# Feed-forward sums moved from GpSimd to VectorE, with a replanned order

## The chip, the core and the metric

The kernel runs on one core of a Trainium2 chip. The metric is the device time of one execution in microseconds, as a median of runs. The engines are TensorE (PE in the profile; its weight loads are PEld), VectorE (DVE), ScalarE (ACT), GpSimd (POOL) and SyncE (SP), whose queue issues the transfers.

## What is computed

One layer of an encoder trunk over 1024 prompt rows and 32 sample rows (1056 in all), width 1024: a pair of recurrent mixers, cross attention, and a gated feed-forward of width 2816, each added to the running rows x. The end of the layer, cut to what this change touches:

```python
x = x + cross_attend(rmsnorm(x, lw['norm_cross']), mk, mv, lw['w_cq'], lw['w_co'])
n = rmsnorm(x, lw['norm_ffn'])
x = x + (jax.nn.silu(n @ lw['w_ff1']) * (n @ lw['w_ff3'])) @ lw['w_ff2']
```

and after it a final RMSNorm. Everything is float32.

## The kernel before

The program is first recorded as a graph: every call on an engine makes a node (`record`), with the tiles it reads and writes. Then `order` plans all of it. It keeps a clock for each engine, gives each node a duration (`price`), a delay between engines (`wait`) and a priority (the longest path to the end, less the node's `bias`, L382 to L385), picks for each engine the ready node with the earliest start and, among those, the highest priority, and places tiles in SBUF regions and PSUM banks as it goes. `LEAD` says how many nodes of earlier phases may be left when a node of a phase is taken. `emit` then issues all nodes in that order from one line, L340, so nearly every row of the profile has that line, and the tiles' names must tell rows apart: `bank` is PSUM; `rw` holds split weights, `wr` and `ma` raw weights; `f`, `ma`, `mb` and `r` hold the rest. SP issues all transfers, in its own order.

A float32 matrix product is done with two float32r parts for each factor: ScalarE rounds a tile to `hi` (CAST in the profile), another engine subtracts to get `lo`, and three matmuls (hi hi, hi lo, lo hi) are added in PSUM for each 128 of the inner dimension.

The phases that matter here:

- **Cross output** (phase 3, end of `cross`): `w_co` in 8 column tiles of 128, 4 row blocks of 264 each. Behind each block `operands` adds x, scales it, stores x to DRAM, and forms what the feed-forward reads: split tiles and, in the manner of Strassen and Winograd, the sums t1 to t4 of its quarters. It also adds up squares; three matmuls with a matrix of ones and a few small operations then give the row scale `rb`.
- **Hidden layer** (phase 4, `ff_hidden`): 11 column blocks of 256 (m), each with two branches, `w_ff1` and `w_ff3`. A branch is seven products (1 to 7) in place of eight; each is 4 inner tiles x 3 matmuls x 2 row halves (s) of 264 rows, so a branch is 168 matmuls and a block 336. `fast_w` loads the raw weights (512 KB twice), makes four weight sums of 128x512 on GpSimd, and for each product a hi (ScalarE) and a lo (VectorE). `fast` issues the matmuls; products 7 and 4, 2 and 3 share PSUM banks, the second adding onto the first after a VectorE sum (128x264, out of PSUM) has read it. At the end of the first branch (`evac1`) come, on 128x1056 tiles, a product with `rb`, a sigmoid, a product with it, and a second product with `rb`; at the end of the second (`evac3`) the product of both branches and four differences of 128x264 for each row half, then stores to DRAM.
- **Second product** (phase 5, `ff_out`): the first 10 hidden blocks, in groups of `FF_GROUPS` pairs, 2 in each of five groups. For each group the operands are loaded and split (128x528, hi on ScalarE, lo on GpSimd and VectorE in turn), then for each of four column tiles (j) seven products of 12 matmuls for each pair, and VectorE adds each out of PSUM to sums in SBUF: 14 sums of 128x264 for each group and j. In group 2 GpSimd adds x, 128x1056 eight times.
- **Tail** (phase 6): the last hidden block by a plain product, then norm and stores.

Of the kernel before, what the change touches and what calls it, by code (L numbers as in the profile page):

```python
# [20 lines left out]
T = TP + NS  # L21
# [13 lines left out]
FF_GROUPS = (2, 2, 2, 2, 2)  # L35
# [16 lines left out]
WAIT, WAIT_PE, SWITCH = 0.0, 0.1, 0.06  # L52
FREE_PS, FREE_SB = 0.2, 0.2
# [7 lines left out]
LEAD = {0: BIG, 1: 1100, 2: 250, 3: 400, 4: 300, 5: 200, 6: 200}  # L61
HOME = {"keep": ("f0", "r0"), "wr": ("wr",), "wh": ("rw",), "wl": ("rw",), "wr2": ("wr",), "wh2": ("rw",), "wl2": ("rw",),
        "op": ("r0", "mb"), "sr": ("wr", "ma"), "sh": ("rw",), "sl": ("rw",), "sh3": ("rw",), "sl3": ("rw",), "sx": ("ma", "f0"),
# [3 lines left out]
FIFO = {"wr": 2, "wh": 2, "wl": 2, "p": 44, "rp": 5, "op": 56, "sr": 2, "sh": 4, "sl": 4, "sx": 4, "sh3": 8, "sl3": 8, "hst2": 4, "xr": 2, "wr2": 4, "wh2": 8, "wl2": 8, "ckv": 7, "mrow": 2}  # L67
# [119 lines left out]
class Node:  # L187
    def __init__(self, graph, eng):
        self.eng, self.i = eng, len(graph.nodes)
        self.calls, self.cost, self.late = [], 0.0, 0.0  # L190
        self.preds, self.bufs, self.unit, self.bias, self.phase = {}, {}, graph.unit, graph.bias, graph.phase
        graph.nodes.append(self)
# [10 lines left out]
def wait(a, b):  # L203
# [42 lines left out]

def change(a, b):

    if a is None:
        return 0.0  # L250
    (_, x, kx), (m, y, ky) = a.calls[-1], b.calls[0]
# [10 lines left out]
class Graph:  # L262
# [36 lines left out]
    def record(self, eng, method, args, kw):  # L299
# [5 lines left out]
        cost, late = price(eng, method, args, kw)  # L305
# [45 lines left out]
    def order(self):  # L351
# [30 lines left out]
        for n in reversed(nodes):  # L382
            n.path = n.cost + n.late + max((s.path + wait(n.eng, s.eng) for s in succs[n]), default=0.0)
# [3 lines left out]
        clock = dict.fromkeys(engines, 0.0)  # L387
        ready = {e: [] for e in engines}
# [122 lines left out]
        def add(n):  # L511
            t = max((when[p] + wait(p.eng, n.eng) for p in n.preds), default=0.0)
# [5 lines left out]
        while len(done) < len(nodes):  # L518
            turn_over()
            best = None  # L520
            for e in engines:
# [7 lines left out]
                for t, n in sorted(ready[e], key=lambda r: (max(r[0], now), -r[1].path)):  # L529
                    t = max(t, now)  # L530
# [19 lines left out]
            clock[e] = start + n.cost  # L550
            when[n] = start + n.cost + n.late
# [36 lines left out]
class Net:  # L588
# [330 lines left out]
    def cross(self):  # L919
# [76 lines left out]
        for m in range(KD):  # L996
            w = self.load_w(self.i["w_co"][0, :, 128 * m:128 * m + 128], KD)
            self.gemm(w, act, KD, self.operands(m, sq), blocks=[(TQ * q, TQ) for q in range(4)])
        self.rstd(sq)

    def operands(self, m, sq):
# [9 lines left out]
        def evac(t0, n, ps):  # L1011
# [8 lines left out]
            if m >= 4 or h == 0:  # L1020
                self.split(hs, ls, x)
            if m < 4 and h == 1:
                t1 = self.t[5, k, s] = new("t1")
                G.tensor_tensor(t1, x, self.x[k, s, 0], ALU.subtract)
            if m >= 4 and h == 1:
                E = V if m == 7 else G
                t2, t3, t4 = self.t[6, k, s], _, self.t[4, k, s] = new("t2"), new("t3"), new("t4")
                E.tensor_tensor(t3, x, self.x[k, s, 1], ALU.subtract)
                self.split(self.xh[:, k, t0:t0 + n], self.xl[:, k, t0:t0 + n], t3)
                E.tensor_tensor(t2, x, self.t[5, k, s], ALU.subtract)  # L1030
                E.tensor_tensor(t4, self.x[m, s, 0], t2, ALU.subtract)
            if m == 0:
                S.activation(sq[:, t0:t0 + n], t, AF.Square)
            else:
                S.activation(t, t, AF.Square)
                G.tensor_tensor(sq[:, t0:t0 + n], sq[:, t0:t0 + n], t, ALU.add)
        return evac
# [16 lines left out]
    def fast_w(self, ap, nk, order, tags, pairs):  # L1054
# [4 lines left out]
        raw = self.wp.tile([128, nk, 2, 256], F32, tag="sr", name="fraw")  # L1059
        if pairs:  # L1060
            nc.sync.dma_start(raw, ap.rearrange("(k e p) m -> p k e m", e=2, p=128))
        else:
            for e in range(2):
                nc.sync.dma_start(raw[:, :, e], ap[128 * nk * e:128 * nk * (e + 1)].rearrange("(k p) m -> p k m", p=128))
        a11, a21, a12, a22 = raw[:, :, 0, 0:128], raw[:, :, 0, 128:256], raw[:, :, 1, 0:128], raw[:, :, 1, 128:256]
# [3 lines left out]
        for i in order:  # L1069
# [5 lines left out]
            hi, lo = (self.wp.tile([128, nk, 128], F32R, tag=tag, name="f" + tag[:2]) for tag in tags)  # L1075
# [4 lines left out]
    def fast(self, ws, act, nk, evac, order):  # L1080
# [721 lines left out]
```

## Time and profile before

| | |
|---|---|
| median of 3 runs | 2042.04 us (2041.89 to 2043.87) |
| profiled execution | 2041.77 us, span 2040.0 us |
| TensorE busy | 1892.7 us (93%) |
| VectorE busy | 1431.3 us (70%) |
| GpSimd busy | 910.2 us (45%) |
| ScalarE busy | 944.9 us (46%) |
| granted TensorE clock, mean | 0.972 |

A row of the stage view reads: stretch, its length, then busy time and number of instructions of PE, PEld, DVE, ACT and POOL, the granted clock, the DMA share and GB/s. A row of the timeline reads: start, length, engine, line, operation, out<-in, shape, count, and in brackets the idle time ahead of it with what ended it. A row of groups has busy time and mean ns behind the count. A row of the waits view says who waited for whom: total us, times, longest. Times are from the start of the span. Busy time of VectorE and GpSimd contains what one of them waits for the other, since an instruction that has started counts.

### The profile page before, as it was taken

What the parts mean: (1) busy time and instruction counts of PE and PEld (TensorE: products, weight loads), DVE (VectorE), ACT (ScalarE), POOL (GpSimd) and SP (SyncE); (2) the same over time, 40 slices, a digit from 0 to 9 for tenths busy, and PEclk for the clock granted to TensorE, in tenths of its full rate; (3) what the DMA queues carried; (4) which work ended last, traced back from release to release, by engine and by line L of the source; (5) the groups of instructions that cost most, each with busy time, mean ns of one, the idle gap of its engine ahead of it and who ended that gap; (6) DMA issues with size and microseconds to landing.
All of it is one profiled execution on the core that took longest, in us unless ns stands there. A gap on an engine that the chain in (4) does not pass through costs nothing. (4 is left out here: it accounts for less than half of the span.)

```text
span 2040.0 us, 40406 instructions
## 1 busy us (share of the span) xinstructions
PE 1892.7 (93%) x15377; PEld 1739.6 (85%) x15377; DVE 1431.3 (70%) x3093; ACT 944.9 (46%) x2454; POOL 910.2 (45%) x1159
## 2 busy tenths in 40 slices
PE   7899999998998999899999997999999999899898
PEld 6878777787877788899999987899999999899897
DVE  4876667767767765645654558776777667889996
ACT  5577537845664766633322345323322222463322
POOL 5742343344435331116200056566566556666742
PEclk9999989999999999899999998999999999999999
DMA  4100101011010112541211122123322224465422
GB/s 138 42 22 25 36 23 32 20 31 32 22 32 18 33 33 69 177 137 42 62 42 42 53 75 74 42 95 105 106 79 80 89 80 138 143 197 159 127 84 96
DMA packets 158179, 149.52 MB, mean 73 GB/s; under 512 B 10144, under 2 KB 146464, under 8 KB 157984
## 3 DMA queue, kind: packets, MB, share of 16 engines
q1 hardware_dynamic: 157984, 146.93, 22.8%
q8 instruction: 121, 1.98, 0.4%
q14 instruction: 74, 0.61, 0.1%
HBM read 111.02 MB, written 35.88 MB: 72 GB/s over the span
## 5 line engine op out<-in xcount | busy, mean ns | idle before, releaser
L340 PE MATMUL bank<-r,rw 128*128 128x264 f32 (+1 forms) x5664 | 914.4, 313 | 32.0 <-DVE rw L340 6.1
L340 PEld LDWEIGHTS bank<-r,rw 128*128 128x128 f32 x5664 | 811.2, 191 | 55.3 <-DVE rw L340 9.0
L340 PE MATMUL bank<-mb,rw 128*128 128x264 f32 (+4 forms) x3600 | 505.0, 296 | 50.0 <-DVE ma L340 19.8
L340 PEld LDWEIGHTS bank<-mb,rw 128*128 128x128 f32 x3600 | 478.1, 192 | 61.5 <-issue 26.0
L340 DVE TENSOR_TENSOR f<-bank,f 128x264 f32<-128x264 f32 (+6 forms) x895 | 321.6, 384 | 163.3 <-PE bank L340 148.5
L340 POOL TENSOR_TENSOR f<-f 128x264 f32<-128x264 f32 (+8 forms) x255 | 240.0, 954 | 303.6 <-ACT f L340 237.9
L340 PE MATMUL bank<-f 128*128 128x64 f16 (+6 forms) x2630 | 297.4, 253 | 35.8 <-DVE f L340 16.1
L340 ACT CAST rw<-wr 128x256 fp32r<-128x256 f32 (+2 forms) x223 | 145.5, 660 | 298.1 <-PE bank L340 171.3
L340 DVE TENSOR_TENSOR rw<-wr,rw 128x256 fp32r<-128x256 f32 (+2 forms) x193 | 178.5, 928 | 68.5 <-ACT rw L340 63.3
L340 PEld LDWEIGHTS bank<-f 128*128 128x128 f32 (+4 forms) x1582 | 165.9, 160 | 65.6 <-DVE f L340 17.9
L340 ACT ACTIVATE f<-f 128x256 f32<-128x256 f32 (+7 forms) x374 | 151.4, 422 | 111.5 <-DVE f L340 89.9
L340 ACT COPY f<-f 64x256 f16<-64x256 f16 (+1 forms) x408 | 149.1, 368 | 46.2 <-DVE f L340 37.9
L340 DVE TENSOR_TENSOR f<-f 128x256 f32<-128x256 f32 (+8 forms) x152 | 115.2, 773 | 27.9 <-ACT f L340 14.8
L340 DVE TENSOR_TENSOR rw<-ma,rw 128x512 fp32r<-128x512 f32 (+1 forms) x86 | 115.6, 1356 | 16.7 <-ACT rw L340 15.3
L340 POOL TENSOR_SCALAR f<-f 128x64 f32<-128x64 f32 (+6 forms) x124 | 54.9, 444 | 157.9 <-DVE f L340 98.2
L340 ACT COPY f<-bank 128x264 f32<-128x264 f32 (+6 forms) x221 | 75.7, 362 | 98.9 <-PE bank L340 80.9
L340 ACT CAST rw<-ma 128x512 fp32r<-128x512 f32 (+1 forms) x86 | 50.9, 598 | 138.9 <-PE bank L340 80.8
L340 POOL TENSOR_TENSOR r<-f,r 128x352 fp32r<-128x352 f32 (+1 forms) x41 | 56.1, 1377 | 67.7 <-ACT r L340 38.1
L340 POOL TENSOR_TENSOR rw<-wr,rw 128x1024 fp32r<-128x1024 f32 x30 | 71.7, 2393 | 29.5 <-ACT rw L340 25.9
L340 PEld LDWEIGHTS <-f 128*128 128x128 f16 x1156 | 52.6, 99 | 35.8 <-issue 8.6
L340 ACT ACTIVATE f<-bank,f 128x256 f32<-128x256 f32 (+4 forms) x122 | 51.0, 431 | 61.9 <-DVE f L340 26.1
L340 PE MATMUL bank<-f,mb 64*64 64x64 f32 (+7 forms) x830 | 74.3, 248 | 1.9 <-DVE f L340 1.1
(180 smaller groups left out, 2292.8 us busy)
## 6 DMA issues: line engine op xcount, KB each, us to landing
wr<-in_w_ff_dram SPq DMA_DIRECT2D x40, 512.0 KB
f<-h_scratch SPq DMA_DIRECT2D x62, 264.0 KB
wr<-in_w_in_dram SPq DMA_DIRECT2D x30, 512.0 KB
ma<-in_w_ff_dram SPq DMA_DIRECT2D x24, 512.0 KB
h_scratch<-f SPq DMA_DIRECT2D x19, 528.0 KB
f<-mix_scratch SPq DMA_DIRECT2D x24, 176.0 KB
x_scratch<-f SPq DMA_DIRECT2D x32, 132.0 KB
mb<-in_x_prompt_dram SPq DMA_DIRECT2D x16, 256.0 KB
```

Of the source, the lines that this page charges most:

```text
L340: getattr(eng, method)(*args, **kw)
```

## The change

- In the hidden layer, GpSimd's products with the sigmoid and with `rb`, and its differences behind `evac3`, go to VectorE. GpSimd keeps the sums of weights.
- In the second product, all operand low parts, the additions of x (now in group 1) and the final additions of the common part go to VectorE; the groups are 3, 3, 2, 2 pairs.
- At the end of the cross output, the differences t1, t2, t3 go to VectorE; t4 and its low part are GpSimd's.
- The first hidden block runs both branches in turn: products 1, 2, 7, 3 of each alternating, then 5, 6, 4 of one and of the other, with a PSUM bank for each product above 2, and its own rule for the sums. The load of its first weights belongs to the phase ahead and follows the sixth of the cross weights.
- hi and lo of a weight or operand are one tile.
- From phase 3 on the planner uses other durations (`close_price`) and delays, and a clock for a port: an operation of GpSimd on two tensors, or one of VectorE with two inputs from SBUF, is not started before the last such one ends. Biases are added; `LATER` puts the elementwise end of a branch 10 us back in priority. `LEAD` of phase 4 falls from 300 to 100.

What this does to the order, at three places. Rows are as the built program has them: number, line, operation, out<-in, shape, count. VectorE in a middle column block of the hidden layer, around the end of the first branch, before:

```order
2173 L340 TENSOR_TENSOR f_0_71<-f_0_71 128x1056
2174 L340 TENSOR_TENSOR f_0_71<-bank_61,f_0_71 128x264
2175 L340 TENSOR_TENSOR f_0_71<-f_0_71 128x1056
2176 L340 TENSOR_TENSOR rw_83<-ma_12981,rw_83 128x512 x2
2177 L340 TENSOR_TENSOR f_0_71<-bank_62,f_0_71 128x264
2178 L340 TENSOR_TENSOR f_0_71<-bank_58,f_0_71 128x264
2179 L340 TENSOR_TENSOR rw_83<-ma_12981,rw_83 128x512
2180 L340 TENSOR_TENSOR f_0_71<-f_0_71 128x1056
2181 L340 TENSOR_TENSOR ma_12981<-bank_63,f_0_71 128x264
```

and now:

```order
2246 L415 TENSOR_TENSOR f_0_71<-f_0_71 128x1056
2247 L415 TENSOR_TENSOR f_0_71<-bank_63,f_0_71 128x264
2248 L415 TENSOR_TENSOR f_0_71<-f_0_71 128x1056
2249 L415 TENSOR_TENSOR rw_83<-ma_12947,rw_83 128x512
2250 L415 TENSOR_TENSOR f_0_71<-f_0_71,ma_12947 128x1056
2251 L415 TENSOR_TENSOR f_0_71<-f_0_71 128x1056
2252 L415 TENSOR_TENSOR f_0_71<-bank_61,f_0_71 128x264
2253 L415 TENSOR_TENSOR f_0_71<-f_0_71 128x1056
2254 L415 TENSOR_TENSOR f_0_71<-bank_62,f_0_71 128x264
2255 L415 TENSOR_TENSOR f_0_71<-f_0_71 128x1056
2256 L415 TENSOR_TENSOR ma_12947<-bank_59,f_0_71 128x264
```

The products with the sigmoid (rows 2250 and 2251) and both second products with `rb` (2253 and 2255) stand between sums out of PSUM.

GpSimd over the same column block, now (before, the three rows of 128x1056 and eight of 128x264 stood among them):

```order
631 L415 TENSOR_TENSOR ma_12947<-wr_75 128x512
632 L415 TENSOR_TENSOR ma_12947<-ma_12947,wr_75 128x512
633 L415 TENSOR_TENSOR wr_75<-wr_75 128x4x128
634 L415 TENSOR_TENSOR ma_12947<-ma_12947,f_0_71 128x4x128
635 L415 TENSOR_TENSOR ma_12947<-ma_12947 128x512
636 L415 TENSOR_TENSOR f_0_71<-ma_12947 128x512
637 L415 TENSOR_TENSOR ma_12947<-ma_12947 128x4x128
638 L415 TENSOR_TENSOR wr_75<-wr_75,ma_12947 128x4x128
```

Only the four weight sums of each branch are left.

TensorE at the end of the cross output (`ma_8341` is its last operand) and the start of the hidden layer (`r_0_79`), with the sums of squares (128x352), before:

```order
4288 L340 MATMUL bank_60<-ma_8341,rw_83 128x264 x6
4289 L340 MATMUL bank_58<-r_0_79,rw_83 128x264 x12
4290 L340 MATMUL bank_59<-r_0_79,rw_83 128x264 x12
4291 L340 MATMUL bank_58<-r_0_79,rw_83 128x264 x6
4292 L340 MATMUL bank_61<-f_0_71 128x352
4293 L340 MATMUL bank_63<-f_0_71 128x352
```

and now:

```order
4288 L415 MATMUL bank_65<-ma_8341,rw_83 128x264 x6
4289 L415 MATMUL bank_63<-r_0_79,rw_83 128x264 x6
4290 L415 MATMUL bank_59<-r_0_79,rw_83 128x264 x6
4291 L415 MATMUL bank_63<-r_0_79,rw_83 128x264 x6
4292 L415 MATMUL bank_59<-r_0_79,rw_83 128x264 x6
4293 L415 MATMUL bank_60<-r_0_79,rw_83 128x264 x6
4294 L415 MATMUL bank_61<-r_0_79,rw_83 128x264 x6
4295 L415 MATMUL bank_63<-r_0_79,rw_83 128x264 x6
```

Rows 4289 to 4292 are product 1 of the first branch, 4293 and 4294 begin product 1 of the second, and 4295 product 2 of the first. The sums of squares come 20 rows of six matmuls after the start.

The diff, cut:

```diff
-FF_GROUPS = (2, 2, 2, 2, 2)
+LATER = 10.0
+FF_GROUPS = (3, 3, 2, 2)
...
-LEAD = {0: BIG, 1: 1100, 2: 250, 3: 400, 4: 300, 5: 200, 6: 200}
+LEAD = {0: BIG, 1: 1100, 2: 250, 3: 400, 4: 100, 5: 200, 6: 200}
...
+def close_price(eng, method, args, kw):
...
+        return 0.065 + n * 1.05e-3 + (0.065 if method == "scalar_tensor_tensor" else 0.0), 0.0
...
+    if method == "tensor_tensor":
+        return 0.13 + n * 2.12e-3 + (0.45 if args[3] == ALU.pow else 0.0), 0.0
...
+def shares_port(eng, method, args):
+    if eng == "gpsimd":
+        return method == "tensor_tensor"
+    if eng != "vector" or method not in ("tensor_tensor", "scalar_tensor_tensor", "tensor_tensor_scan", "copy_predicated"):
+        return False
+    return sum(isinstance(v, View) and v.buf.space == "SB" and math.prod(v.shape[1:]) > 1 for v in args[1:]) >= 2
...
+                    t = max(t, now, port) if n.port else max(t, now)
...
+            if n.port:
+                port = clock[e] - (0.15 if e == "gpsimd" else 0.0)
...
+            if m == 5:
+                self.late = nc.nodes[-1]
...
-                G.tensor_tensor(t1, x, self.x[k, s, 0], ALU.subtract)
+                V.tensor_tensor(t1, x, self.x[k, s, 0], ALU.subtract)
-                E = V if m == 7 else G
                 t2, t3, t4 = self.t[6, k, s], _, self.t[4, k, s] = new("t2"), new("t3"), new("t4")
-                E.tensor_tensor(t3, x, self.x[k, s, 1], ALU.subtract)
+                V.tensor_tensor(t3, x, self.x[k, s, 1], ALU.subtract)
                 self.split(self.xh[:, k, t0:t0 + n], self.xl[:, k, t0:t0 + n], t3)
-                E.tensor_tensor(t2, x, self.t[5, k, s], ALU.subtract)
-                E.tensor_tensor(t4, self.x[m, s, 0], t2, ALU.subtract)
+                V.tensor_tensor(t2, x, self.t[5, k, s], ALU.subtract)
+                G.tensor_tensor(t4, self.x[m, s, 0], t2, ALU.subtract)
...
+        if first:
+            nc.phase -= 1
...
+        if first:
+            for node in nc.nodes[-2:]:
+                node.preds[self.late] = None
...
-            hi, lo = (self.wp.tile([128, nk, 128], F32R, tag=tag, name="f" + tag[:2]) for tag in tags)
+            w = self.wp.tile([128, 2, nk, 128], F32R, tag=tag, name="fw")
+            hi, lo = w[:, 0], w[:, 1]
...
+            bank = i if alone and i > 2 else " aadcdbc"[i]
...
+                elif m:
+                    V.tensor_tensor(o[:, {7: 2, 4: 1, 3: 3}[i]], ps, c, ALU.add)
+                elif i == 4:
+                    V.tensor_tensor(o[:, 1], ps, o[:, 1], ALU.add)
+                    V.tensor_tensor(o[:, 1:4], o[:, 1:4], c.unsqueeze(1).to_broadcast([128, 3, TQ]), ALU.add)
                 else:
+                    S.copy(o[:, 2 if i == 7 else 3], ps)
+                    if i == 7:
+                        S.copy(o[:, 1], ps)
+            final = 3 if m else 4
...
+                    nc.bias = self.turn + LATER
...
-                    G.tensor_tensor(t, t, sg, ALU.mult)
-                    (G if s else V).tensor_tensor(th, th, r, ALU.mult)
+                    V.tensor_tensor(t, t, sg, ALU.mult)
+                    V.tensor_tensor(th, th, r, ALU.mult)
...
-                    G.tensor_tensor(y[:, 2], x[:, 3], x[:, 0], ALU.subtract)
-                    G.tensor_tensor(y[:, 0], x[:, 2], y[:, 2], ALU.subtract)
-                    G.tensor_tensor(y[:, 1], x[:, 2], x[:, 3], ALU.subtract)
-                    G.tensor_tensor(y[:, 3], x[:, 1], y[:, 0], ALU.subtract)
+                    V.tensor_tensor(y[:, 2], x[:, 3], x[:, 0], ALU.subtract)
+                    V.tensor_tensor(y[:, 0], x[:, 2], y[:, 2], ALU.subtract)
+                    V.tensor_tensor(y[:, 1], x[:, 2], x[:, 3], ALU.subtract)
+                    V.tensor_tensor(y[:, 3], x[:, 1], y[:, 0], ALU.subtract)
...
+                order = [(f, i) for i in (1, 2, 7, 3) for f in range(2)] + [(f, i) for f in range(2) for i in (5, 6, 4)]
+                jobs = [(self.fast_w(self.i[name][0, :, cs], 4, order, f, "sh", False, f == 0), evac)
+                        for f, (name, evac) in enumerate((("w_ff1", evac1), ("w_ff3", evac3)))]
+                self.fast(jobs, act, 4, order, True)
...
-                    (V if k % 2 else G).tensor_tensor(lo, raw, hi.bitcast(F32), ALU.subtract)
+                    V.tensor_tensor(lo, raw, hi.bitcast(F32), ALU.subtract)
...
-                    (V if n == 2 else G).tensor_tensor(dst, dst, common[j][:, s], ALU.add)
+                    V.tensor_tensor(dst, dst, common[j][:, s], ALU.add)
...
+                w = self.fast_w(self.i["w_ff2"][0, rows, 256 * j:256 * j + 256], n, jobs, 0, "sh3", True)
...
-                if g == 2:
+                if g == 1:
...
-                        G.tensor_tensor(acc[m], acc[m], x, ALU.add)
+                        V.tensor_tensor(acc[m], acc[m], x, ALU.add)
```

More of the change, by code (lines that the diff above doesn't have):

```diff
@@ L191, in __init__ @@
         self.preds, self.bufs, self.unit, self.bias, self.phase = {}, {}, graph.unit, graph.bias, graph.phase
+        self.close, self.port = graph.phase >= CLOSE, False
         graph.nodes.append(self)
@@ L200, in __getattr__, with wait @@
         return lambda *args, **kw: self.graph.record(self.name, method, args, kw)
-def wait(a, b):
+def wait(n, s):
+    a, b = n.eng, s.eng
+    if s.close:
+        return 0.0 if a == b else DELAY.get((a, b), DELAY[a])
     if a == b:
@@ L304, in record @@
         self.open = node if eng == "tensor" else None
-        cost, late = price(eng, method, args, kw)
+        cost, late = (close_price if node.close else price)(eng, method, args, kw)
+        node.port = node.close and shares_port(eng, method, args)
         node.cost, node.late = node.cost + cost, max(node.late, late)
@@ L382, in order @@
         for n in reversed(nodes):
-            n.path = n.cost + n.late + max((s.path + wait(n.eng, s.eng) for s in succs[n]), default=0.0)
+            n.path = n.cost + n.late + max((s.path + wait(n, s) for s in succs[n]), default=0.0)
         for n in nodes:
@@ L387, in order @@
         clock = dict.fromkeys(engines, 0.0)
+        port = 0.0
         ready = {e: [] for e in engines}
@@ L511, in add @@
         def add(n):
-            t = max((when[p] + wait(p.eng, n.eng) for p in n.preds), default=0.0)
+            t = max((when[p] + wait(p, n) for p in n.preds), default=0.0)
             ready[n.eng].append((t, n))
@@ L1052, in halves, with fast_w @@
         return v[:, :, 0], v[:, :, 1]
-    def fast_w(self, ap, nk, order, tags, pairs):
+    def fast_w(self, ap, nk, order, job, tag, pairs, first=False):
         nc = self.nc
@@ L1059, in fast_w @@
         raw = self.wp.tile([128, nk, 2, 256], F32, tag="sr", name="fraw")
+        phase = nc.phase
+        if first:
+            nc.phase -= 1
         if pairs:
@@ L1068, in fast_w @@
         G.tensor_tensor(s2, s1, a11, ALU.subtract)
-        for i in order:
+        for i in [i for f, i in order if f == job]:
             if i == 7:
@@ L1078, in fast_w, with fast @@
             yield hi, lo
-    def fast(self, ws, act, nk, evac, order):
+    def fast(self, jobs, act, nk, order, alone=False):
         nc = self.nc
         ps = {}
-        for i in order:
+        for f, i in order:
+            ws, evac = jobs[f]
+            self.turn += 0.73 * nk
             nc.bias = self.turn
-            self.turn += 0.73 * nk
             hi, lo = next(ws)
-            bank = " aadcdbc"[i]
-            fresh = (bank, 0) not in ps
+            bank = i if alone and i > 2 else " aadcdbc"[i]
+            fresh = (f, bank, 0) not in ps
             for s in range(2):
+                nc.bias = self.turn
                 if fresh:
-                    ps[bank, s] = self.psg.tile([128, TQ], F32, tag="g", name="ps_f")
-                p = ps[bank, s]
+                    ps[f, bank, s] = self.psg.tile([128, TQ], F32, tag="g", name="ps_f")
+                p = ps[f, bank, s]
                 for k in range(nk):
@@ L1129, in ff_hidden @@
             cs = slice(256 * m, 256 * m + 256)
-            order = (1, 6, 7, 5, 4, 2, 3) if m else (1, 2, 7, 5, 3, 6, 4)
-            out, u, full = [[None, None], [None, None]], [None, None], [False, False]
+            out, u = [[None, None], [None, None]], [[None, None], [None, None]]
             def sums(f, i, s, ps):
@@ L1196, in ff_out @@
         order = (1, 6, 7, 5, 2, 4, 3)
+        jobs = [(0, i) for i in order]
         acc = [fp.tile([128, T], F32, tag="ac", name="acc") for _ in range(KD)]
@@ L1229, in ff_out @@
             for j in range(4):
[L1230 to L1232 removed]
+                w = self.fast_w(self.i["w_ff2"][0, rows, 256 * j:256 * j + 256], n, jobs, 0, "sh3", True)
+                self.fast([(w, partial(evac, g, j))], act, n, jobs)
+                if g == 1:
                     for m in (2 * j, 2 * j + 1):
```

107 lines of the change are left out of this document (79 added, 28 removed).

## The prediction

> **What bounds the kernel now.** I read the busy shares first, then the span cut into its stages, then what TensorE waited for in each stage, then one such wait step by step.
>
> ```profile
> PE 1892.7 (93%) x15377; PEld 1739.6 (85%) x15377; DVE 1431.3 (70%) x3093; ACT 944.9 (46%) x2454; POOL 910.2 (45%) x1159
> 975.00:1134.00 159.00, 157.67 (x916) 145.47 (x915) 85.84 (x234) 44.64 (x118) 7.00 (x7) 1.00 0.16 48
> 1134.00:1195.00 61.00, 60.28 (x456) 57.50 (x455) 31.98 (x77) 22.91 (x56) 13.68 (x14) 1.00 0.22 68
> 1195.00:1257.00 62.00, 52.05 (x390) 51.11 (x389) 43.53 (x61) 27.96 (x69) 39.37 (x40) 0.89 0.19 61
> 1257.00:1319.00 62.00, 49.57 (x345) 46.44 (x344) 49.92 (x80) 29.45 (x68) 31.80 (x22) 0.92 0.20 60
> 1319.00:1769.00 450.00, 423.08 (x3363) 417.39 (x3362) 321.30 (x397) 133.64 (x254) 282.43 (x199) 0.98 0.30 100
> 1769.00:1998.00 229.00, 212.46 (x1686) 207.07 (x1685) 218.30 (x423) 96.23 (x241) 141.97 (x131) 1.00 0.44 136
> 1998.00:2040.00 42.00, 32.87 (x215) 28.49 (x213) 26.55 (x51) 11.23 (x36) 9.91 (x30) 0.92 0.28 104
> 1360.00:1380.00 20.00, 20.00 (x167) 20.00 (x166) 10.80 (x17) 4.06 (x9) 10.97 (x11) 1.00 0.20 68
> ```
>
> TensorE is the bound overall. The last row is a stretch without a gap: 20/167 = 0.12 us from matmul to matmul. Against that pace 1195 to 1319 (end of the cross output, first column block of the hidden layer) holds 735 matmuls, 88 us of work in 124, so 36 lost. The other ten hidden column blocks, 1319 to 1769, hold 3363, 403 us in 450: 47 lost. The second product, 1769 to 1998, holds 1686, 202 us in 229: 27 lost. These 110 us are what the change can reach; from 975 to 1195 TensorE has no gap to give. VectorE is busy 218 of 229 us in the second product.
>
> ```profile
> PE bank L340 <- DVE ma L340: 16.6, 8, 2.9
> PE bank L340 <- DVE f L340: 4.7, 2, 2.7
> PE bank L340 <- ACT rw L340: 3.8, 8, 1.0
> PE bank L340 <- DVE rw L340: 1.7, 8, 0.2
> 1476.19 2.79 POOL L340 TENSOR_TENSOR f<-f,ma 128x1056 f32<-128x1056 f32 x1 [6.13 <-ACT ma L340]
> 1476.54 5.86 DVE L340 TENSOR_TENSOR rw<-ma,rw 128x512 fp32r<-128x512 f32 x2
> 1478.94 5.81 POOL L340 TENSOR_TENSOR f<-f 128x1056 f32<-128x1056 f32 x2
> 1483.01 2.29 DVE L340 TENSOR_TENSOR rw<-ma,rw 128x512 fp32r<-128x512 f32 x1
> 1485.23 2.33 DVE L340 TENSOR_TENSOR f<-f 128x1056 f32<-128x1056 f32 x1
> 1487.48 0.42 DVE L340 TENSOR_TENSOR ma<-bank,f 128x264 f32<-128x264 f32 x1
> 1488.05 3.17 PE L340 MATMUL bank<-mb,rw 128*128 128x264 f32 x24 [1.97 <-DVE ma L340]
> 1493.09 0.68 DVE L340 TENSOR_TENSOR rw<-f,rw 128x512 fp32r<-128x512 f32 x1
> ```
>
> The first four rows are TensorE's waits from 1319 to 1769: 26.8 us, 21.3 of them for a VectorE sum out of PSUM. The rest is one of them. GpSimd has three 1056-element products in a row; VectorE's low parts of weights, 0.68 us alone (last row), take 2.93 each until those are through, so the sum of product 7 ends at 1487.90, and product 4, which adds onto the same bank, waits 1.97 us. It comes back once a column block. So operations that read two SBUF tensors on VectorE wait out GpSimd's, one by one; those that read PSUM do not (0.42).
>
> By the Trainium skill (SBUF — State Buffer, "Who interferes with whom") a VectorE instruction with two SBUF inputs and a GpSimd instruction that reads SBUF exclude each other; the 2.93 against 0.68 agrees.
>
> **Steady hidden blocks.** Prices alone, and group means:
>
> ```profile
> 1460.12 1.26 DVE L340 TENSOR_TENSOR ma<-ma,f 128x1056 f32<-128x1056 f32 x1
> 1267.66 0.42 DVE L340 TENSOR_TENSOR f<-f 128x264 f32<-128x264 f32 x1
> 1488.66 1.28 POOL L340 TENSOR_TENSOR wr<-wr 128x512 f32<-128x512 f32 x1
> 1461.46 0.76 POOL L340 TENSOR_TENSOR f<-ma 128x264 f32<-128x264 f32 x1 [5.06 <-DVE ma L340]
> L340 POOL TENSOR_TENSOR f<-f 128x1056 f32<-128x1056 f32 x19 | 54.1, 2869 | 0.0
> ```
>
> One column block is 336 matmuls, 40.3 us. VectorE now: 14 low parts x 0.68, 20 PSUM sums x 0.42, five 1056 products x 1.26: 24.2 us. GpSimd: 8 weight sums x 1.28, 8 differences x 0.76, three products x 2.87: 24.9. The change moves three products and eight differences: VectorE 24.2 + 3 x 1.26 + 8 x 0.42 = 31.3, GpSimd 10.2. Over ten blocks VectorE was busy 321, 32.1 a block: 7.9 us more than its 24.2, waited on GpSimd, 0.32 of GpSimd's 24.9. With the same share VectorE is at 31.3 + 0.32 x 10.2 = 34.6 of 40.3; with every GpSimd operation waited out it is at 41.5, just over TensorE. The first is nearer: the order puts GpSimd's sums singly, and no long product is left in its queue. So TensorE stays the bound. Of the 47 lost, the PSUM waits fall from 21.3 to 4, the weight waits from 5.5 to 4. The clock, mean 0.98, cost 0.02 x 450 = 9.
>
> ```profile
> 1575.00:1579.00 4.00, 2.98 (x14) 3.02 (x15) 2.31 (x6) 1.07 (x2) 2.89 (x2) 0.57 0.00 0
> ```
>
> It halves right behind the longest gaps, as here, so 3 remain; of the other 11, small gaps, 9. That leaves 20: **27 us gained** (10 if every GpSimd operation is waited out, 38 at the floor).
>
> **Second product.**
>
> ```profile
> 1840.43 0.41 DVE L340 TENSOR_TENSOR rw<-wr,rw 128x256 fp32r<-128x256 f32 x1
> L340 DVE TENSOR_TENSOR r<-ma,r 128x528 fp32r<-128x528 f32 x1 | 0.7, 696 | 0.0
> L340 DVE TENSOR_TENSOR f<-bank,f 128x264 f32<-128x264 f32 x162 | 63.9, 420 | 1.0 <-PE bank L340 0.9
> L340 POOL TENSOR_TENSOR r<-f,r 128x528 fp32r<-128x528 f32 x17 | 25.4, 1496 | 9.7 <-ACT r L340 9.7
> L340 POOL TENSOR_TENSOR wr<-wr 128x256 f32<-128x256 f32 x17 | 14.5, 852 | 0.3
> ```
>
> Groups of 3, 3, 2, 2 pairs in place of five of 2 save 56 VectorE sums out of PSUM (240 to 184, 23.5 us), and VectorE takes 35 operand low parts x 0.70, 16 sums x 0.42 and eight 1056 sums x 1.26 of x: 41 us. The first two groups: 8 x 126 matmuls, 121 us. VectorE's order there has about 70 sums x 0.42, 48 operand parts x 0.70, 55 parts of weights of 384 columns (0.55, between 0.41 and 0.68) and a few more: 106; with 0.32 of GpSimd's 32 sums of about 1 us it comes to 116, under TensorE. I take 125. The last two groups: 8 x 84 matmuls, 81 us. VectorE has 112 x 0.42, 51 x 0.41, 13 x 0.70, 18 final sums x 0.42, and five long ones: 91. So here VectorE becomes the bound, 91 + 0.32 x 32 x 0.74 (GpSimd's 256-column sums alone, an estimate from 0.85 contended) = 99. Together 224 against 229: **5 gained** (212 with no waiting, 253 with all).
>
> **Boundary.** Before:
>
> ```profile
> 1257.35 3.10 PE L340 MATMUL bank<-r,rw 128*128 128x264 f32 x24
> 1264.46 1.32 PE L340 MATMUL bank<-r,rw 128*128 128x264 f32 x6 [4.01 <-ACT f L340]
> 1244.20 0.93 SPq L340 DMA_DIRECT2D wr<-in_w_ff_dram  x2
> 1248.30 0.62 ACT L340 CAST rw<-wr 128x512 fp32r<-128x512 f32 x1 [1.38 <-DMA wr<-in_w_ff_dram]
> ```
>
> The stop at 1264 comes after product 1 alone, 24 matmuls. After the change both branches share the first block, so two products 1 stand there and products 5, 6, 4, whose operands come last, follow eight others; the three sum-of-squares matmuls follow 120 matmuls of the feed-forward, not 30. Against that, product 1 of the second branch needs weights whose transfer goes into a region that opens when the cross output has ended: by the rows above 4 us from issue to ScalarE, then 0.62 and 0.68, against 2.9 us of product 1: some 2 to 5 us of stop, and VectorE has a queue of about 25 short operations (10 us) from the last output blocks. VectorE takes 20 differences x 0.42 = 8.4 there and gives GpSimd 8 operand parts; GpSimd loses about as many longer ones. Of 36 lost I take 22: **14 gained** (0 to 24). The first transfer issued a phase early gains nothing: on SP it still stands behind the last cross weights, and behind 23 stores of x where it stood behind 27.
>
> The cross stage is reordered too, since prices change from there; TensorE was full, so 0 (3 either way). The tail gets six more sums: **1 lost**.
>
> Sum: 27 + 5 + 14 - 1 = 45. The profiled execution took 2041.8 us, 1.8 more than its span and 0.3 under the median of the runs: 2042 - 45 = **1997 us**.
>
> **Rivals.** *TensorE's floor*: no term waits, 38 + 17 + 24 - 1 = 78: 1964. For it: VectorE still has 15% free in the hidden blocks. Against: the second product. *VectorE becomes the bound*, since most GpSimd operations are waited out (share 0.8): 31.3 + 8.2 = 39.5 a block still fits, 22 gained; the second product 106 + 26 and 91 + 19 = 242, 13 lost; boundary 8: 2042 - 16 = 2026. For it: VectorE at 218 of 229 there already. *Nothing gained*: both engines' work is one queue at the port, whichever of them does it (share 1): hidden 10, second product -24, boundary 14: 2042. The rows speak against it, as the work halves on its way (2.87 to 1.26, 0.76 to 0.42). By the Trainium skill (Perfetto Trace Analysis, "Optimizing Scalar/DVE Operations") moving work between GpSimd and VectorE might not help, as they share a read port; no run here shows it yet. *Slower*: GpSimd starves at the port. Its chain of four weight sums a branch waits each time for a 1.26 product, weights are late, TensorE waits 2 x 1.26 in each of 22 blocks: 55 us over the forecast's gain of 45, and ten halved clock stretches at 1.7: 2042 - 45 + 55 + 17 = 2069. It decides from 45/22 = 2 us a block. Against it: GpSimd is free three quarters of the time, and weights are ordered several products ahead.
>
> **How the numbers follow.** Forecast 0.50, floor 0.20, VectorE bound 0.18, nothing 0.06, slower 0.06. Range 1966 to 2030: the floor's edge and the VectorE case with 4 to spare; the last two and the extreme of the floor stay out. Differences under 0.2% (4 us) count as no change here: faster 0.88, same 0.06, slower 0.06.
>
> **What would show it.** Right: no 2.9 us low parts of weights in the hidden blocks, GpSimd busy under 650 us, the recurring 2 us wait gone, columns of 41 to 42 us, VectorE without idle in the last two groups. Wrong: TensorE waiting on low parts or weight sums in most blocks, the first two groups over 130 us, or a stop over 8 us behind the first product 1.

## Result and profile after

The changed kernel takes 1986.03 us (1981.37 to 1989.32), against 2042.95 for the kernel before: ratio 0.9715, 95% interval 0.969 to 0.974. That is 57 us gained where 45 were forecast (1997), inside the range of 1966 to 2030. The profiled execution took 1989.3, with a span of 1987.6.

The stages below are cut in one profiled execution of each kernel, where TensorE starts the first matmul of each stage. The "last four tiles" are the last four of the cross output's eight column tiles, 384 of its 768 matmuls; the expectations further down call them its last third.

| stage | before, us | after, us | gained | forecast |
|---|---|---|---|---|
| up to the cross stage | 975.5 | 980.3 | -4.8 | 0 |
| cross stage up to its last four tiles | 220.2 | 222.0 | -1.8 | 0 |
| last four tiles of the cross output | 61.7 | 46.7 | 15.0 | 14 with the next row |
| first hidden column block | 61.9 | 59.9 | 2.0 | |
| ten other hidden column blocks | 449.9 | 421.1 | 28.8 | 27 |
| second product and tail | 270.8 | 257.6 | 13.2 | 4 |
| span | 2040.0 | 1987.6 | 52.4 | 45 |

The first row is taken for scatter and not for an effect of the change: in both traces every engine's instructions come in the same order up to 861 us, the profiled runs with the changed planner (below) have 971 to 980 in this row, and the profiled execution is 3.3 us over the median of its kernel.

Busy shares of the changed kernel, its stages (columns as in the prediction), and TensorE's waits in the ten blocks (1309 to 1730) and in the second product (1730 to 1945):

```profile
PE 1883.4 (95%) x15377; PEld 1737.4 (87%) x15377; DVE 1399.1 (70%) x3200; ACT 950.2 (48%) x2430; POOL 662.7 (33%) x952
1202.30:1249.00 46.70, 46.70 (x386) 46.70 (x385) 30.78 (x71) 24.46 (x61) 19.77 (x22) 1.00 0.28 90
1249.00:1308.90 59.90, 51.68 (x344) 49.03 (x343) 44.89 (x78) 32.27 (x81) 35.18 (x31) 0.86 0.22 65
1308.90:1730.00 421.10, 415.04 (x3362) 411.52 (x3361) 334.95 (x516) 137.55 (x252) 139.30 (x77) 1.00 0.30 102
1730.00:1863.50 133.50, 127.37 (x1011) 125.78 (x1009) 107.46 (x190) 68.40 (x148) 39.94 (x34) 0.97 0.59 177
1863.50:1945.00 81.50, 81.50 (x669) 81.29 (x668) 81.23 (x200) 30.58 (x72) 25.07 (x30) 1.00 0.39 115
```

```profile
PE bank L415 <- DVE rw L415: 4.8, 7, 2.6
PE bank L415 <- DVE ma L415: 0.5, 1, 0.5
```

```profile
PE bank L415 <- ACT r L415: 2.9, 1, 2.9
PE bank L415 <- DVE rw L415: 2.6, 3, 1.4
```

GpSimd is busy for 248 us less, VectorE for 32 less although it took over the work, and TensorE's waits in the ten blocks fell from 26.8 us to 5.3. The recurring stop has gone. One place in a middle block, VectorE first, then TensorE:

```profile
1420.80 2.34 DVE L415 TENSOR_TENSOR f<-f 128x1056 f32<-128x1056 f32 x1
1423.06 0.42 DVE L415 TENSOR_TENSOR f<-bank,f 128x264 f32<-128x264 f32 x1
1423.40 2.01 DVE L415 TENSOR_TENSOR f<-f 128x1056 f32<-128x1056 f32 x1
1425.34 0.42 DVE L415 TENSOR_TENSOR f<-bank,f 128x264 f32<-128x264 f32 x1
1425.68 2.00 DVE L415 TENSOR_TENSOR f<-f 128x1056 f32<-128x1056 f32 x1
1427.60 0.42 DVE L415 TENSOR_TENSOR ma<-bank,f 128x264 f32<-128x264 f32 x1
```

```profile
1424.96 3.68 PE L415 MATMUL bank<-mb,rw 128*128 128x264 f32 x26
1429.01 1.25 PE L415 MATMUL bank<-mb,rw 128*128 128x264 f32 x8 [0.36 <-DVE rw L415]
```

Beside them GpSimd has three of its weight sums in a row:

```profile
1419.85 2.18 POOL L415 TENSOR_TENSOR ma<-wr 128x512 f32<-128x512 f32 x1 [13.49 <-DVE rw L415]
1422.10 2.20 POOL L415 TENSOR_TENSOR ma<-ma,wr 128x512 f32<-128x512 f32 x1
1424.26 2.31 POOL L415 TENSOR_TENSOR wr<-wr 128x512 f32<-128x512 f32 x1
```

VectorE's products still wait for them (2.0 to 2.3 us where 1.26 is the length alone), but each stands between sums out of PSUM, and TensorE stops for 0.36 us where it stopped for 1.97.

The last two groups of the second product (1863.5 to 1945) are the row to keep in mind: VectorE busy 81.23 of 81.50 us, and TensorE without a gap all the same.

### The profile page after: what moved, and what is told of

Its sections match the earlier page's. It is cut to its first block, busy times and chain, and to the rows that moved or that the text cites. A ratio compares the mean times of both kernels' runs of the same rounds, so it can differ in the third digit from the quotient of the medians.

```text
span 1987.6 us, 40211 instructions
## 1 busy us (share of the span) xinstructions
PE 1883.4 (95%) x15377; PEld 1737.4 (87%) x15377; DVE 1399.1 (70%) x3200; ACT 950.2 (48%) x2430; POOL 662.7 (33%) x952
## 5 line engine op out<-in xcount | busy, mean ns | idle before, releaser
L415 PE MATMUL bank<-mb,rw 128*128 128x264 f32 (+3 forms) x3456 | 485.7, 294 | 12.6 <-DVE rw L415 8.8
L415 DVE TENSOR_TENSOR f<-bank,f 128x264 f32<-128x264 f32 (+8 forms) x905 | 327.4, 385 | 167.6 <-PE bank L415 151.8
L415 PE MATMUL bank<-f 128*128 128x64 f16 (+7 forms) x2639 | 295.5, 252 | 36.8 <-DVE f L415 17.2
L415 ACT CAST rw<-wr 128x1024 fp32r<-128x1024 f32 (+3 forms) x183 | 132.7, 730 | 225.7 <-PE bank L415 146.5
L415 POOL TENSOR_TENSOR f<-f 128x2 f32<-128x2 f32 (+7 forms) x161 | 104.3, 658 | 306.1 <-ACT f L415 233.3
L415 DVE TENSOR_TENSOR f<-f 128x264 f32<-128x264 f32 (+8 forms) x252 | 185.5, 750 | 23.9 <-ACT f L415 15.0
L415 DVE TENSOR_TENSOR rw<-wr,rw 128x512 fp32r<-128x512 f32 (+3 forms) x153 | 130.8, 859 | 52.4 <-ACT rw L415 51.5
L415 ACT CAST rw<-ma 128x512 fp32r<-128x512 f32 (+2 forms) x124 | 70.9, 573 | 154.7 <-POOL ma L415 85.7
L415 DVE TENSOR_TENSOR rw<-ma,rw 128x512 fp32r<-128x512 f32 (+2 forms) x124 | 81.0, 660 | 36.5 <-ACT rw L415 36.4
L415 POOL TENSOR_TENSOR ma<-ma 128x512 f32<-128x512 f32 (+2 forms) x37 | 51.8, 1402 | 90.6 <-DVE rw L415 88.9
```

Of the source, the lines that this page charges most:

```text
L415: getattr(eng, method)(*args, **kw)
```

## Experiments

Each run's time, and its profile cut in the same way; "ten blocks" starts at the second hidden column block. In e2, e6 and e10 some of the second product's first matmuls run ahead of the hidden layer's last ones, so in all runs "ten blocks" ends when 3360 matmuls have run since its start, which in the others is the start of the second product. The stages are those of one execution each; where the order is the same, as in the changed kernel and e5 up to the second product, they agree within 0.5 us.

| kernel | median, us | ratio to before, 95% | last four tiles | first block | ten blocks | rest |
|---|---|---|---|---|---|---|
| before | 2042 to 2044 | | 61.7 | 61.9 | 449.9 | 270.8 |
| after | 1986.0 | 0.9715 (0.9690 to 0.9740) | 46.7 | 59.9 | 421.1 | 257.6 |
| e1, hidden work back | 2013.2 | 0.9860 (0.9839 to 0.9881) | 52.9 | 61.2 | 429.7 | 261.4 |
| e2, moves alone | 2044.9 | 1.0007 (0.9992 to 1.0023) | 53.5 | 69.1 | 457.3 | 269.8 |
| e3, no port in hidden layer | 1992.0 | 0.9752 (0.9728 to 0.9776) | 48.9 | 59.6 | 425.5 | 255.5 |
| e4, old durations | 2001.7 | 0.9805 (0.9783 to 0.9828) | 50.8 | 60.3 | 422.3 | 270.1 |
| e5, groups of two | 1984.1 | 0.9711 (0.9694 to 0.9729) | 46.7 | 59.9 | 420.7 | 258.5 |
| e6, second product back | 1988.9 | 0.9730 (0.9714 to 0.9747) | 46.7 | 59.9 | 421.5 | 260.2 |
| e7, no turns | 1980.3 | 0.9690 (0.9676 to 0.9705) | 46.7 | 59.1 | 416.9 | 257.1 |
| e8, t1 to t3 back | 1981.1 | 0.9695 (0.9678 to 0.9712) | 47.1 | 61.0 | 420.2 | 258.0 |
| e9, LATER at 0 | 2000.3 | 0.9786 (0.9772 to 0.9801) | 46.7 | 57.2 | 436.8 | 255.3 |
| e10, moves and LATER | 2010.2 | 0.9832 (0.9810 to 0.9854) | 52.2 | 67.2 | 428.8 | 267.7 |
| e11, LATER alone | 2024.6 | 0.9909 (0.9893 to 0.9925) | 60.9 | 61.9 | 432.0 | 271.9 |
| e12, no turns, LATER 20 | 1967.5 | 0.9626 (0.9609 to 0.9643) | 46.7 | 58.3 | 409.6 | 257.0 |

### Engine or order: e1 to e4

The prediction's reason for the hidden layer is theory A: the moves shorten what VectorE waits for GpSimd, so the sum behind product 7 is in time. The rival, B, is the new planner.

**e1**, the hidden layer's work back on GpSimd, in the changed kernel:

```diff
-                    V.tensor_tensor(t, t, sg, ALU.mult)
-                    V.tensor_tensor(th, th, r, ALU.mult)
+                    G.tensor_tensor(t, t, sg, ALU.mult)
+                    (G if s else V).tensor_tensor(th, th, r, ALU.mult)
...
-                    V.tensor_tensor(y[:, 2], x[:, 3], x[:, 0], ALU.subtract)
+                    G.tensor_tensor(y[:, 2], x[:, 3], x[:, 0], ALU.subtract)
```

and so for the other three differences.

> The changed kernel, with the hidden layer's three 1056-element products and eight differences of each column block back on GpSimd; the new planner orders them. Theory A (engine): the 29 us gained in the ten steady column blocks come from which engine does the work, since each GpSimd operation holds VectorE up by about 0.4 of its length, 92 us of such waits in all before and 42 now. Then these blocks go back from 421 us to 440 to 450, and the kernel to 2005 to 2015. Rival B (order): they come from a planner that knows the real durations and the shared port, and so puts the sums out of PSUM ahead of what stalls them. Then the blocks stay at 421 to 428 and the kernel at 1983 to 1995.

**e2**, the same lines the other way round, in the kernel before.

> The kernel before, with its old planner, and only the hidden layer's products and differences moved from GpSimd to VectorE. A (engine): the ten steady column blocks fall from 450 us to 421 to 430, the kernel from 2042 to 2012 to 2022, the boundary and the second product stay as before. B (order): the old planner still puts VectorE's sums out of PSUM behind long operations; 440 to 450 and 2032 to 2045.

**e3**, in the changed kernel:

```diff
-        node.port = node.close and shares_port(eng, method, args)
+        node.port = node.close and self.phase in (3, 5, 6) and shares_port(eng, method, args)
```

> The changed kernel, whose planner doesn't know the shared port in the hidden layer (it does in the other phases), with all else as changed. A (engine): hardly a difference, steady blocks 421 to 426, kernel 1983 to 1992. B (order), if it is the port's clock: 435 to 450, kernel 2000 to 2015.

**e4**, in the changed kernel:

```diff
-CLOSE = 3
+CLOSE = 99
```

> The changed kernel, planned throughout with the old durations and delays and without the port; its biases, lead and interleaved first block stay. A (engine): steady blocks 421 to 430, kernel 1985 to 2000. B (order): steady blocks 435 to 450, boundary and second product lose as well, 5 us each; kernel 2010 to 2030.

e1 gives back 8.6 of the 28.8 us in the ten blocks, which is neither theory; the kernel is within A's 2005 to 2015 only because the boundary and the rest lose 11 us with it, and the cross stage ahead of them 4. Its sum behind product 7 is late again, but by less than before:

```profile
PE bank L415 <- DVE ma L415: 10.2, 6, 1.7
```

e2 refutes A as it stands: the moves alone gain nothing, in those blocks (457.3 against 449.9) or in all. VectorE's wait for GpSimd did shrink in e2: over the two-tensor operations of these blocks, recorded length less the shortest usual one of its shape comes to 92 us before and 38 in e2. TensorE's waits of e2 in these blocks, up to the first matmul of the second product, and one of them on VectorE and TensorE:

```profile
PE bank L340 <- DVE rw L340: 30.5, 11, 3.1
```

```profile
1474.02 1.82 DVE L340 TENSOR_TENSOR f<-f 128x1056 f32<-128x1056 f32 x1
1475.76 2.35 DVE L340 TENSOR_TENSOR f<-f,ma 128x1056 f32<-128x1056 f32 x1
1478.15 4.69 DVE L340 TENSOR_TENSOR f<-f 128x1056 f32<-128x1056 f32 x3
1482.76 0.76 DVE L340 TENSOR_TENSOR f<-bank,f 128x264 f32<-128x264 f32 x2
1483.44 0.42 DVE L340 TENSOR_TENSOR ma<-bank,f 128x264 f32<-128x264 f32 x1
1483.78 0.68 DVE L340 TENSOR_TENSOR rw<-ma,rw 128x512 fp32r<-128x512 f32 x1
```

```profile
1484.51 1.69 PE L340 MATMUL bank<-mb,rw 128*128 128x264 f32 x6 [3.09 <-DVE rw L340]
```

The five long products, now all VectorE's, stand in a row from 1474.02 to 1482.84, and the low part that TensorE needs is behind them. The wait for a sum out of PSUM (21.3 us of 26.8 before) has become a wait for low parts (30.5). By the Trainium skill (Perfetto Trace Analysis, "Optimizing Scalar/DVE Operations") moving work between these two engines might not help; e2 agrees, 1.0007, though the reason seen here is the order and not the port.

B falls for the hidden layer too: e4, with the old durations and no port clock, has 422.3 there. What e4 shares with the changed kernel and e2 does not is the biases, `LATER` above all, `LEAD` and the turns. The expectations of e3 and e4 for A hold for the ten blocks (425.5, 422.3), but not as evidence for A alone. The port's clock is worth 4.4 us there once the new durations are in use; e4 without either is no worse than the changed kernel.

### What turns the moves into a gain: e9 to e11

Theory C: `LATER`, which puts the elementwise end of a branch 10 us back in priority, does. Rival D: the planner's durations.

**e9**, in the changed kernel:

```diff
-LATER = 10.0
+LATER = 0.0
```

> The changed kernel with LATER at 0: the elementwise end of a branch is no longer put 10 us back in priority; moves, durations and port clock stay. Theory C (priority): the moves alone gained nothing since VectorE takes its long products in a row ahead of low parts, and LATER is what turns the moves into a gain. Then the ten steady column blocks go from 421 us back to 438 to 452, with TensorE waiting over 15 us for low parts, and the kernel to 2003 to 2018. Rival D (durations): with the real durations and the port's clock the planner places the products well without it: 421 to 428, kernel 1984 to 1994.

**e11**, in the kernel before (the same lines in `evac3`, and the bias set back ahead of the next row half), and **e10**, which is e11 with the moves of e2:

```diff
                 if i == order[-1]:
+                    nc.bias = nc.bias + 10.0
                     t, sg = out[0][s], self.ap.tile([128, 4, TQ], F32, tag="ft4", name="sg")
```

> The kernel before with only the ends of the branches 10 us back in priority; GpSimd keeps its products and differences. C (priority): about what the new planner got without the moves, 428 to 436 for the steady blocks, kernel 2020 to 2032, with the sum behind product 7 still late by about 2 us in each block. If moves and priority only work together (each removes one of two waits in a row): 443 to 452, kernel 2036 to 2046.

> The kernel before with two things of the change: the hidden layer's products and differences on VectorE, and the ends of its branches 10 us back in priority; old durations, no port clock. C (priority): steady blocks 421 to 430 where the moves alone had 452, kernel 2010 to 2022. D (durations): 440 to 452, kernel 2035 to 2047.

TensorE's waits in the ten blocks, of e9, of e11 and of e10 (up to the first matmul of the second product), each in its own fence, and the stage row of e11:

```profile
PE bank L415 <- DVE rw L415: 18.7, 11, 3.8
PE bank L415 <- DVE f L415: 2.1, 1, 2.1
```

```profile
PE bank L340 <- DVE ma L340: 12.6, 8, 1.7
PE bank L340 <- DVE f L340: 4.1, 2, 2.4
PE bank L340 <- DVE rw L340: 1.6, 2, 1.4
```

```profile
PE bank L340 <- DVE f L340: 4.6, 8, 0.9
PE bank L340 <- DVE rw L340: 4.0, 11, 0.5
```

```profile
1319.20:1751.20 432.00, 413.67 (x3362) 411.16 (x3361) 324.17 (x396) 135.54 (x254) 295.05 (x199) 1.00 0.31 104
```

C holds in all three; e9's 436.8 and 2000 us lie a little under its ranges. In e10 the last of the ten blocks has a stop of 5.24 us for a low part, behind the second product's first matmuls. So the pieces are compared over the first nine blocks, 3024 matmuls with none of the second product among them:

| planner and all else | neither | moves | LATER | both |
|---|---|---|---|---|
| as before | 402.8 | 408.7 (e2) | 385.2 (e11) | 380.1 (e10) |
| as changed | not run | 394.5 (e9) | 388.7 (e1) | 379.8 (after) |

`LATER` alone gains 17.6 us. Over the ten blocks the waits fall from 26.8 to 18.3. The granted clock, which the trace of before has at 0.50 for 17.1 us of them, behind or in stops of 1.9 to 2.9 us, is at 0.50 for 3.4 us in e11, where the eight stops for product 4 take 1.7 us each: some 7 us more of work at full clock. The moves are worth nothing without `LATER` (6 us lost) and 5 to 9 with it. With the work still on GpSimd (e1, e11) the stop before product 4 stays; the moves cut it to 0.9 us or less (e10), and in the changed kernel it is gone. What else was changed (durations, port clock, `LEAD`, turns) gains 14 us where `LATER` is missing (408.7 to 394.5), and which of these does it was not tested; with moves and `LATER` both in it gains nothing (380.1 and 379.8, and 380.3 with the old durations, e4).

### The second product: e5 and e6

**e5**, groups of two, and **e6**, which adds GpSimd's old share:

```diff
-FF_GROUPS = (3, 3, 2, 2)
+FF_GROUPS = (2, 2, 2, 2, 2)
...
-                    V.tensor_tensor(lo, raw, hi.bitcast(F32), ALU.subtract)
+                    (V if k % 2 else G).tensor_tensor(lo, raw, hi.bitcast(F32), ALU.subtract)
...
-                    V.tensor_tensor(dst, dst, common[j][:, s], ALU.add)
+                    (V if n == 2 else G).tensor_tensor(dst, dst, common[j][:, s], ALU.add)
...
-                        V.tensor_tensor(acc[m], acc[m], x, ALU.add)
+                        G.tensor_tensor(acc[m], acc[m], x, ALU.add)
```

> The changed kernel with five groups of two pairs in the second product; its operations stay on VectorE. It adds 56 VectorE sums out of PSUM. Theory S (starts): in a full stretch VectorE starts a 128x264 sum every 0.34 us, though its record is 0.42 long, so VectorE has work for 19 us more, still under TensorE's 205 us: second product and tail 257 to 264 us (257.6 with groups of three), kernel 1984 to 1994. Rival R (records): by record lengths VectorE is over TensorE in every group of two: 24 us more, 272 to 285, kernel 2002 to 2014.

> The changed kernel with the second product as before in both respects: five groups of two pairs, and every other operand low part, the sums of x and two of three final sums on GpSimd; only the planner's durations and port are new there. If groups and moves gained the 13 us: second product and tail back to 268 to 274 us, kernel 1997 to 2006. If the new durations gained them, as the run with the old durations suggests (270.1 with groups and moves as changed): 256 to 262, kernel 1984 to 1992.

The second product of e5, and eight microseconds of VectorE in the changed kernel's last groups:

```profile
1725.20:1941.00 215.80, 209.05 (x1676) 207.59 (x1675) 204.23 (x470) 99.66 (x238) 70.92 (x79) 0.98 0.48 147
```

```profile
1904.10 0.76 DVE L415 TENSOR_TENSOR f<-bank,f 128x264 f32<-128x264 f32 x2
1904.78 0.69 DVE L415 TENSOR_TENSOR r<-ma,r 128x528 fp32r<-128x528 f32 x1
1905.40 0.76 DVE L415 TENSOR_TENSOR ma<-bank,ma 128x264 f32<-128x264 f32 x2
1906.08 0.69 DVE L415 TENSOR_TENSOR r<-ma,r 128x528 fp32r<-128x528 f32 x1
1906.70 0.76 DVE L415 TENSOR_TENSOR ma<-bank,ma 128x264 f32<-128x264 f32 x2
```

Two sums take 0.76, not 0.84: where VectorE has work ready it starts a sum every 0.34 us, and a record runs 0.08 into the next. Groups of two cost VectorE 15 us more of busy time (204 against 189 in 1730 to 1945) and the kernel nothing (258.5 against 257.6). Theory S holds; groups of three are worth nothing here. Nor are the moves worth much: over ten blocks and rest together e6 has 681.7, e5 679.2, the changed kernel 678.7, before 720.7. Most of the 13 us comes from the new durations: with the old ones (e4, groups and moves as changed) the rest is 270.1, as before, and with the new ones but the old groups and engines (e6) it is 260.2, in the range of the second reading. "Durations" means durations, delays and port clock here: e4 takes all three away, and they were not told apart for this stage.

### The boundary: e7 and e8

**e7**, the branches of the first block one after the other:

```diff
-                order = [(f, i) for i in (1, 2, 7, 3) for f in range(2)] + [(f, i) for f in range(2) for i in (5, 6, 4)]
+                order = [(f, i) for f in range(2) for i in (1, 2, 7, 3, 5, 6, 4)]
```

> The changed kernel with the first column block's branches one after the other (1, 2, 7, 3, 5, 6, 4 of the first, then of the second) in place of in turn. If taking turns is what gained at the boundary (106.6 us from the last third of the cross output to the second column block, 123.6 before): a stop behind four products of the first branch, boundary 114 to 122, kernel 1994 to 2002. Rival: the boundary was gained at the end of the cross output (46.7 us there against 61.7) by the differences on VectorE and the order, and turns are worth little: 106 to 110, kernel 1984 to 1990.

**e8**, the differences back on GpSimd:

```diff
-                V.tensor_tensor(t1, x, self.x[k, s, 0], ALU.subtract)
+                G.tensor_tensor(t1, x, self.x[k, s, 0], ALU.subtract)
...
-                V.tensor_tensor(t3, x, self.x[k, s, 1], ALU.subtract)
+                E = V if m == 7 else G
+                E.tensor_tensor(t3, x, self.x[k, s, 1], ALU.subtract)
...
-                V.tensor_tensor(t2, x, self.t[5, k, s], ALU.subtract)
+                E.tensor_tensor(t2, x, self.t[5, k, s], ALU.subtract)
```

> The changed kernel with the differences t1, t2 and t3 of the cross output back on GpSimd. If it is the engine: GpSimd's runs of 128x264 operations hold up VectorE's low parts and with them the last weights again, and the last third of the cross output goes from 46.7 us back to 54 to 62, kernel 1993 to 2002. If it is the order (the last weights' parts ahead of the ends of the output blocks, as the planner now places them): 46 to 51, kernel 1983 to 1991.

Neither carries the boundary. The two kernels were faster than any reading had it, e7 with 1980 us by 4 and e8 with 1981 by 2. Without turns the first block is as long (59.1), and the block behind it takes 41.6 us; in the changed kernel that block takes 45.7, with a stop of 2.6 us for a low part that ends at 1320.8. With the differences on GpSimd the boundary is 108.1 against 106.6.

The 15 us lie at the end of the cross output. There, in the kernel before, the last column tile's weights, on ScalarE, VectorE and TensorE (in each fence an operation before them, then their own or the stops for them):

```profile
1230.96 0.52 ACT L340 ACTIVATE f<-f 128x264 f32<-128x264 f32 x1 [16.74 <-DVE f L340]
1240.32 1.03 ACT L340 CAST rw<-wr 128x1024 fp32r<-128x1024 f32 x1
```

```profile
1230.02 0.43 DVE L340 TENSOR_TENSOR f<-bank,r 128x264 f32<-128x264 f32 x1 [11.94 <-PE bank L340]
1242.76 1.42 DVE L340 TENSOR_TENSOR rw<-wr,rw 128x1024 fp32r<-128x1024 f32 x1
```

```profile
1241.40 0.81 PE L340 MATMUL bank<-mb,rw 128*128 128x264 f32 x2 [3.45 <-ACT rw L340]
1244.23 2.13 PE L340 MATMUL bank<-mb,rw 128*128 128x264 f32 x8 [2.02 <-DVE rw L340]
```

ScalarE and VectorE had stood idle for 16.7 and 11.9 us up to 1231; then the ends of the tiles ahead went first on both, and the rounding of the last weights came at 1240, behind them. That order explains only part of the stop. In the built program the rounding also waits for the last matmul that reads the space it writes, and by the trace that one ended at 1237.2: TensorE had worked on the two column tiles ahead together (120 matmuls in a row on `mb` up to 1229, where one tile has 72) and gave the first room for weights back only then. So the rounding is held up for 3.1 us by ScalarE's queue, and until 1237 by TensorE's order and the room for weights. After the change TensorE ends one tile of such a pair some 3 us before the other: ScalarE rounds the last two tiles' weights at 1222.83 and 1225.74, with nothing queued ahead (it had idled for 2.45 and 0.42 us, waiting for TensorE), and the stretch has no gap (46.70 of 46.70).

What of the change put it right isn't settled. The old durations (e4) leave 50.8, the differences' engine hardly matters (e8), the hidden layer's work back on GpSimd costs 6 (52.9 in e1), and moves in the hidden layer alone already change this place (53.5 in e2, 52.2 in e10): biases, `LEAD` and durations were not told apart.

### A faster version: e12

e7 and `LATER` at 20.0.

> The changed kernel without turns in the first column block and with the branches' ends 20 us back in priority in place of 10. If what is left in the steady blocks (about 0.5 us a block behind the sum of product 7) is still the branches' ends: 412 to 416 us for them, kernel 1972 to 1979. If 10 us already puts them behind all that TensorE waits for: 416 to 421, kernel 1978 to 1986; if too late, the second product's first operands come late and its first column goes from 22 us to over 26.

The ten blocks and, for them, the whole stage row:

```profile
1301.90:1711.40 409.50, 409.50 (x3361) 409.50 (x3361) 326.13 (x515) 135.89 (x246) 140.83 (x81) 1.00 0.33 107
```

TensorE has no gap in 410 us: 0.1219 us a matmul, a block every 41.0, less than the 412 to 416 expected. The first column of the second product takes 19.8 us (22.7 in the changed kernel), so its operands don't come later. At 1967.5 us, under the 1972 expected, it beats both kernels; its interval lies clear of the changed kernel's.

## Why the prediction was right, and where it wasn't

- **The bound.** The forecast lay 12 us low, with its bound right and each of its three gains put down to a cause that the runs bear out in part or not at all. TensorE stayed the bound, as said, and "VectorE becomes the bound" fell: VectorE is full in the last two groups and holds nothing up. TensorE's floor was about where it was put: e12's ten blocks are at 409.6, and its kernel 1967.5 against the 1964 of that rival.
- **Steady hidden blocks, +27 forecast, +28.8 measured.** The size held, the cause only in part, so that the size came out so near is partly luck. The step that failed is "the order puts GpSimd's sums singly, and no long product is left in its queue. So TensorE stays the bound", by which the moves themselves took the waits away. The moves alone are worth nothing, `LATER` alone 18, the moves on top 5 to 9. Nor do GpSimd's sums come singly: three stand in a row from 1419.85 to 1426.57. I listed `LATER` among the changes and gave it no term. VectorE's own queue, into which the three products went, was the place to look: the rival of a new wait in place of the old was argued for GpSimd's weight sums and not for low parts behind VectorE's products, which e2 shows (30.5 us). The share of GpSimd's time that VectorE waits came out at 42 us of 101 by the same comparison with the shortest lengths, 0.42, and 92 of 244 before, 0.38; I took 0.32, with 2.87 us as the price of a GpSimd product alone, which is a mean with waits in it (the shortest takes 2.43). The low end of 10 us has no working: 41.5 us a block makes 415 for ten, 35 under 450.
- **Second product, +5 and tail -1 forecast, +13.2 in all.** The mis-sized term is the 99 us for the last two groups ("So here VectorE becomes the bound"), measured 81.5. The recorded lengths of VectorE's 199 operations there add up to 96.7, close to that sum; about 0.077 us for each is overlap of neighbours, 15 us, and some 81.5 is left. By the Trainium skill (Perfetto Trace Analysis, "Optimizing Scalar/DVE Operations") a profiled VectorE length holds about twice the fixed overhead, since the half for the acknowledged write runs beside the next instruction; the rows above agree: from 264 to 528 columns the time from start to start goes from 0.34 to 0.62 us and the record from 0.42 to 0.69, which leaves a fixed part of 0.06 us in the one and 0.14 in the other, an estimate from these two lengths. The prediction should have used it. The first two groups took 133.5, not 125, over the 130 that I had named as a sign of error: 7 us at the start, with 2.9 of it a wait for the rounding of the first operands, and 3 in the last column before the third group. And most of the gain has another source than named: the planner's durations, not groups and moves. The tail's -1 was right (42.6 against 42.0).
- **Boundary, +14 forecast, +17.0 measured.** Right in size by luck, wrong in place: the first block, to which turns and the later sums of squares belong, gained 2.0 of it, and e7 has the same without turns (59.1) and shows that they cost some 4 in the block behind. The stop of some 2 to 5 us came, on TensorE in two pieces, 3.14 for the first branch's low part and 1.30 for the second branch's rounding. That low part's rounding had ended at 1246.4, and it stood in VectorE's queue, behind the work from the cross output, until 1251.9:

```profile
1252.58 4.05 PE L415 MATMUL bank<-r,rw 128*128 128x264 f32 x22 [3.14 <-DVE rw L415]
1257.93 4.34 PE L415 MATMUL bank<-r,rw 128*128 128x264 f32 x16 [1.30 <-ACT rw L415]
```

The cross output's 15 us were in the 36 lost that the prediction counted, but none of its steps was about them.
- **Nothing gained** fell for the change and holds for its moves alone; **slower** fell: TensorE's waits in the ten blocks come to 5.3 us, where that rival needs 2 in each of 22 branches.

Of the signs named: no low part of weights takes 2.9 us any more, the recurring stop has gone, columns take 41.2 to 42.3 after the first (45.7), VectorE has no idle time in the last two groups; GpSimd is at 663, just over the 650.

## What to carry to other kernels

Work moved to another engine lands in that engine's order: ask what stands behind it there and who waits for that, before counting what it no longer blocks. Where a planner sets the order, a one-line bias can be worth more than the moves that the diff is named for, so each such line gets its own term. A size that comes out near does not show the cause: cut the runs by stage and take the pieces out singly. For a full engine, cost an instruction by the time from one start to the next in a stretch without gaps, not by the length of its record, and don't read a busy share near 100% as the bound while TensorE has no gap.

## What the runs showed that I had not expected

- VectorE at 99.7% busy (81.23 of 81.50) beside TensorE with no gap: both limits met in the same stretch.
- In a stretch of 410 us TensorE ran 3360 matmuls of 128x264 at 0.1219 us each, with a granted clock of 1.00 (e12), while VectorE and GpSimd still held each other up: VectorE's waits for GpSimd, 38 us there by the comparison with the shortest lengths, cost TensorE nothing, since they fell on work that was not due.
- A change in the hidden layer alone took 8 us off the end of the cross output (61.7 to 53.5 in e2), and put 7 on the first column block (61.9 to 69.1): the planner's priorities reach across stages, so that a test of one part in such a kernel has to be read stage by stage.
